# A two-block hybrid transformer on one core: transfer, rounding and subtraction of each piece of weights a thousand instructions ahead in the scheduler's order of preference

## The chip, the cores and the metric

The kernel runs on one core of a Trainium2 chip. The time is the device time of one execution in microseconds (us), lower is better; 2093.95 us is the median of three runs of the kernel before. The engines are named as in the profile: PE (TensorE, the matrix multiplier; PEld is its loading of the stationary operand), DVE (VectorE), ACT (ScalarE), POOL (GpSimd) and SP (SyncE, which here issues all the transfers of weights). Each engine executes its own instructions strictly in the order in which the program lists them.

## What is computed

A sequence of 256 tokens of width 1024 goes through a first block of two layers and a second block of one; everything is float32 and the batch is 1. Cut to what matters:

```python
def first_block(x, mem, ...):
    for l in range(2):
        x = x + 0.5 * swiglu(rms_norm(x, ffn1_norm[l]), ffn1_w_in[l], ffn1_w_out[l])
        z = rms_norm(x, mix_norm[l]) @ mix_w_in[l]      # Fox, MoBA and RWKV-7 heads
        y = concat([fox_mixer(z_fox), rwkv7_mixer(z_rwkv), moba_mixer(z_moba)])
        x = x + y @ mix_w_out[l]
        x = x + memory_cross_attention(rms_norm(x, ...), rms_norm(mem, ...), ...)
        x = x + 0.5 * swiglu(rms_norm(x, ffn2_norm[l]), ffn2_w_in[l], ffn2_w_out[l])
    return x

def second_block(x, c, ctx, ...):
    sh1, sc1, g1, sh2, sc2, g2 = split(silu(c) @ w_mod + b_mod, 6)
    p = modulate(rms_norm(x), sh1, sc1) @ w_in           # attention, delta rule, gates
    attn = latent_attention(q, [k_ctx, k], [v_ctx, v])
    gdn = gated_delta_rule_both_directions(ctx, x)       # solves triangular systems by chunk
    x = x + g1 * (merge(attn, gdn) @ w_out)
    x = x + g2 * conv_ffn(modulate(rms_norm(x), sh2, sc2), w_up, conv_w, conv_b, w_down)
    return rms_norm(x, final_norm_w)
```

The inner width of the FFNs is 2816. Nearly all bytes read are weights, each used once.

## The kernel before, in words

**Pieces of weights.** A product with weights is made from pieces of 128 x 1024 float32 numbers, 512 KB each. `piece` (L383) makes one: `raw` (L373) has SP issue the transfer (L375) into one of four `raw` buffers; ScalarE rounds it to the multiplier's format into `wh` (its instruction has L324, `act`), and VectorE subtracts to get the rest, `wl` = raw - wh (L327, `tt`). `wh` and `wl` have three buffers each. Activations are split in the same way, `xTh` and `xTl`, and PE adds up three products for one: xh.wh + xl.wh + xh.wl (L351, `mm`), 24 matmuls of 256 columns to a piece where the activations are stationary or moving in that width. There are 546 pieces.

**Who uses them.** `gemm_tok` (L403) and `gemm_chan` (L434, called in pairs by `gemm_pair`, L446) take a piece right before the matmuls that use it; `mix_out` (L855) does so for the mixers' output. A flag and a queue in `turn` let one product go after another.

**The order of the work.** The program is written as generators that yield estimated times (`merge`, L204ff; `START`, `PACE`), which sets the order in which instructions are handed to a scheduler. The scheduler then lists each engine's instructions by its own estimate of when their operands are ready; among those that are ready the earlier in the program has preference. `high_priority(offset=n)` shifts this preference of the enclosed instructions n instructions forward. Buffers still have to come free: a new `wh` waits until PE has read the third one before it.

**Stages.** A first FFN (with the modulation of block 2's vectors and the cross-attention's keys as side work: sums `macc`, loads `wm`), mixer 0, cross-attention 0, FFN, FFN (with block 2's context as side work), mixer 1, cross-attention 1 and FFN (again with modulation), then block 2: projections, the delta rule in four head groups and attention, the merge, and the convolution FFN. In the mixers and in the delta rule `inverse` (L676) inverts unit triangular matrices of 128: VectorE shuffles (L701) into `iv_tz`, a loop of 15 products `iv_p` and sums `iv_x`, masks into `gW`, `rW` or `iv_tz` and transposes (L720), then PE and ScalarE steps. The delta rule's next group waits for the inverse of the one before (`inv0`, `inv1`, ...). `gcv` are the sums of its short convolution; each reads a PSUM bank that a product has filled.

**The start.** `Builder.__init__` issues the four quarters of `x` (L295), the identity (the first 128 columns of `fconst`, L297) and the first norm's gains (`prm`, L298). PE transposes `x` with the identity (L354), ScalarE and VectorE split it into `xTh` and `xTl`, and the first product begins.

Of the kernel before, what the change touches and what calls it, by code (L numbers as in the profile page):

```python
# [10 lines left out]
F32 = mybir.dt.float32  # L11
F32R = mybir.dt.float32r
# [15 lines left out]
START = (7.0, 9.0, 29.0, 9.0, 85.0, 15.0, 47.0)  # L28

PACE = (2.2, 2.7)  # L30

WM = 4

# [242 lines left out]
class Builder:  # L276
# [104 lines left out]
        s.ts(out, out, 0.5, 0.5, OP.mult, OP.add)  # L381

    def piece(s, src, n):  # L383
        r = s.raw(src, n)
        h = s.stage.tile([128, 1024], F32R, name="wh", bufs=3)
        l = s.stage.tile([128, 1024], F32R, name="wl", bufs=3)
        s.act(h[:, :n], r[:, :n])
        s.sub(l[:, :n], r[:, :n], h[:, :n].bitcast(F32))
        return h, l

    def turn(s):
# [1159 lines left out]
    def gdn_group(s, e, ec, X, hp, latent, S, o, flags, spare):  # L1551
# [56 lines left out]
        def inv():  # L1608
# [30 lines left out]
            a.update(W=W, DT=DT)  # L1639
            yield from s.inverse(e, N, W, (True, False), (1.0, 1.0) if latent else PACE)  # L1640
            flags.add(f"inv{hp}")
# [457 lines left out]
```

## Time and profile before

| | |
|---|---|
| three runs | 2092.67, 2093.95, 2097.84 us |
| the profiled execution | 2097.77 us, of which 2095.9 us are the profile's span |
| PE busy | 2006.1 us (96%) |
| DVE busy | 1604.1 us (77%) |
| ACT busy | 1113.9 us (53%) |
| mean granted clock of PE | 0.974 of full speed |
| transfers | 317.16 MB, mean 151 GB/s |

PE's busy time counts a matmul from its start to its modelled end, so 96% does not mean that it runs at its peak. The idle time of an engine is put down to what released the instruction that ended it, its releaser. Where the granted clock is under 1, matmuls of a stretch ran partly at the lower of the two levels, 1.2 instead of 2.4 GHz.

### The profile page before, as it was taken

How to read it: one execution, taken by the hardware profiler on the slowest of the kernel's cores; microseconds unless marked ns; L12 is line 12 of the kernel's file. 1: busy time of each engine (PE TensorE's matmuls, PEld its weight loads, DVE VectorE, ACT ScalarE, POOL GpSimd, SP SyncE). 2: the span in 40 equal slices, each digit the busy share in tenths (PEclk: the TensorE clock that was granted, in tenths of full speed). 3: DMA queues.
4: the chain of work that ended last, by engine and by line, in shares of the span. 5: the costliest groups of instructions: out<-in, count | busy, mean ns of one | idle time of the engine just before them, and what ended most of it. 6: DMA issues, size and time to landing. Idle time of an engine off the chain costs nothing.

```text
span 2095.9 us, 37277 instructions
## 1 busy us (share of the span) xinstructions
PE 2006.1 (96%) x14344; PEld 1778.8 (85%) x14344; DVE 1604.1 (77%) x3828; ACT 1113.9 (53%) x2057; POOL 14.9 (1%) x16
## 2 busy tenths in 40 slices
PE   8999999999999999999999979999889999999998
PEld 8899878778989889898888758999678888878996
DVE  7978688677786969686787678766688887767985
ACT  6544555476455555464554354444546664546663
POOL 0000000000000000000000000000000000000000
PEclk9999999999999999999988988999989999999999
DMA  8775432154554545554432167665431123554663
GB/s 296 243 231 174 154 113 90 54 172 133 171 160 152 154 148 160 153 164 145 150 111 71 44 234 245 210 193 173 140 111 61 51 62 110 174 168 163 194 194 126
DMA packets 90568, 317.16 MB, mean 151 GB/s; under 512 B 10388, under 2 KB 12952, under 8 KB 90008
## 3 DMA queue, kind: packets, MB, share of 16 engines
q1 hardware_dynamic: 90392, 314.80, 47.5%
q8 instruction: 112, 1.84, 0.4%
q14 instruction: 64, 0.52, 0.1%
HBM read 313.72 MB, written 1.05 MB: 150 GB/s over the span
## 4 chain that ended last, share of the span: by engine, by line
PE 77%; DVE 16%; ACT 4%; issue 2%; DMA 0%; SPq 0%; DVEq 0%; ACTq 0%
PE b L351 73%; DVE wl L327 4%; PE b L354 3%; ACT wh L324 1%; DVE iv_x L348 1%; DVE iv_tz L701 1%; DVE iv_p L327 1%; DVE macc L345 1%; DVE gcv L345 1%; DVE sg L327 1%; ACT sq L324 1%; ACT iv_c L324 0%; DVE iv_tz L327 0%; DVE sg L345 0%; ACT fcb L324 0%
## 5 line engine op out<-in xcount | busy, mean ns | idle before, releaser
L324 ACT ACTIVATE wh<-raw 128x1024 fp32r<-128x1024 f32 (+1 forms) x546 | 569.0, 1043 | 604.4 <-PE b L351 443.2
L327 DVE TENSOR_TENSOR wl<-raw,wh 128x1024 fp32r<-128x1024 f32 (+1 forms) x546 | 654.6, 1204 | 262.3 <-ACT wh L324 241.2
L351 PE MATMUL b<-xTh,wh 128*128 128x256 f32 x2200 | 627.8, 286 | 2.9 <-ACT xTh L324 2.7
L351 PE MATMUL b<-xTh,wl 128*128 128x256 f32 x2200 | 621.9, 283 | 2.1 <-DVE xTl L345 1.2
L351 PE MATMUL b<-xTl,wh 128*128 128x256 f32 x2200 | 621.5, 283 | 0.2
L351 PEld LDWEIGHTS b<-xTh,wh 128*128 128x128 f32 x2200 | 418.2, 190 | 8.7 <-ACT xTh L324 4.5
L351 PEld LDWEIGHTS b<-xTh,wl 128*128 128x128 f32 x2200 | 418.8, 190 | 4.5 <-DVE wl L327 1.6
L351 PEld LDWEIGHTS b<-xTl,wh 128*128 128x128 f32 x2200 | 419.5, 191 | 2.9 <-DVE xTl L345 0.7
L351 PE MATMUL b<-wh,gh 128*128 128x512 f32 x440 | 175.9, 400 | 0.2 <-DVE gcv L345 0.2
L351 PE MATMUL b<-wl,gh 128*128 128x512 f32 x440 | 173.4, 394 | 0.1
L351 PE MATMUL b<-wh,gl 128*128 128x512 f32 x440 | 173.4, 394 | 0.0
L351 PE MATMUL b<-wh,xTh 128*128 128x512 f32 x400 | 161.6, 409 | 7.4 <-DVE iv_x L348 5.0
L351 PE MATMUL b<-wh,xTl 128*128 128x512 f32 x400 | 162.6, 406 | 0.0
L351 PE MATMUL b<-wl,xTh 128*128 128x512 f32 x400 | 159.9, 401 | 1.3 <-DVE wl L327 1.3
L351 PEld LDWEIGHTS b<-wl,gh 128*128 128x128 f32 x440 | 83.2, 189 | 19.0 <-DVE wl L327 0.6
L351 PEld LDWEIGHTS b<-wh,xTh 128*128 128x128 f32 x400 | 75.8, 191 | 27.6 <-issue 7.7
L351 PEld LDWEIGHTS b<-wh,gh 128*128 128x128 f32 x440 | 83.3, 189 | 18.2 <-ACT wh L324 0.6
L351 PEld LDWEIGHTS b<-wh,gl 128*128 128x128 f32 x440 | 83.3, 189 | 17.1
L351 PEld LDWEIGHTS b<-wl,xTh 128*128 128x128 f32 x400 | 76.3, 191 | 17.8 <-DVE wl L327 2.3
L351 PEld LDWEIGHTS b<-wh,xTl 128*128 128x128 f32 x400 | 76.6, 191 | 16.5 <-issue 2.3
L345 DVE SCALAR_TENSOR_TENSOR macc<-wm,mcs,macc 128x512 f32<-128x512 f32 x112 | 82.4, 744 | 0.3
L324 ACT ACTIVATE iv_tz<-b 128x256 f32<-128x256 f32 (+3 forms) x52 | 19.7, 380 | 66.0 <-PE b L351 65.7
(609 smaller groups left out, 3107.1 us busy)
## 6 DMA issues: line engine op xcount, KB each, us to landing
raw<-in_f1i_dram SPq DMA_DIRECT2D x88, 512.0 KB, 4.0
raw<-in_f2i_dram SPq DMA_DIRECT2D x88, 512.0 KB, 4.0
wm<-in_wmod_dram SPq DMA_DIRECT2D x48, 512.0 KB, 4.7
raw<-in_wup_dram SPq DMA_DIRECT2D x44, 512.0 KB, 4.3
raw<-in_f1o_dram SPq DMA_DIRECT2D x40, 512.0 KB, 3.6
raw<-in_wi_q_dram SPq DMA_DIRECT2D x40, 512.0 KB, 3.9
raw<-in_f2o_dram SPq DMA_DIRECT2D x40, 512.0 KB, 3.6
raw<-in_wi_a_dram SPq DMA_DIRECT2D x32, 512.0 KB, 3.9
```

The lines of the kernel that those rows point to most:

```text
L324: return s.nc.scalar.activation(out, in_, func, scale=scale, bias=bias, **kw)
L327: return s.nc.vector.tensor_tensor(out, a, b, op=op)
L345: return s.nc.vector.scalar_tensor_tensor(out, a, sc, b, op0=op0, op1=op1)
L348: s.nc.vector.tensor_reduce(out, in_, axis=AX.X, op=op)
L351: s.last_mm = s.nc.tensor.matmul(out, lhsT, rhs, start=start, stop=stop).ins
L354: s.nc.tensor.transpose(out, in_, s.c("ident"))
L701: nc.vector.stream_shuffle(AR[:, j, :, j:], NC[:, :, j:], [j] * 16 + [16 + j] * 16)
```

## The change

Transfer, rounding and subtraction of a piece are put in a block with a preference of 1000 instructions. What is computed and the buffers stay the same; lines behind the new ones move by two (up to `piece`) and by four (behind it).

```diff
 PACE = (2.2, 2.7)
+
+AHEAD = 1000
...
     def piece(s, src, n):
-        r = s.raw(src, n)
-        h = s.stage.tile([128, 1024], F32R, name="wh", bufs=3)
-        l = s.stage.tile([128, 1024], F32R, name="wl", bufs=3)
-        s.act(h[:, :n], r[:, :n])
-        s.sub(l[:, :n], r[:, :n], h[:, :n].bitcast(F32))
+
+        with s.tc.high_priority(offset=AHEAD):
+            r = s.raw(src, n)
+            h = s.stage.tile([128, 1024], F32R, name="wh", bufs=3)
+            l = s.stage.tile([128, 1024], F32R, name="wl", bufs=3)
+            s.act(h[:, :n], r[:, :n])
+            s.sub(l[:, :n], r[:, :n], h[:, :n].bitcast(F32))
         return h, l
```

SP's queue at the start of the program; `raw` are the pieces, `x` the input, the first `fconst` the identity, the first `prm` the first norm's gains. Before:

```order
L295 DMA x<-in_x_dram 128x512 x2
L297 DMA fconst<-in_fconst_dram 128x128
L298 DMA prm<-in_prm_dram 128x8
L295 DMA x<-in_x_dram 128x512 x2
L375 DMA raw<-in_f1i_dram 128x1024 x5
L301 DMA fconst<-in_fconst_dram 128x1318
L375 DMA raw<-in_f1i_dram 128x1024
L302 DMA prm<-in_prm_dram 128x510
L305 DMA uraw<-in_uconst_dram 128x1024
L307 DMA pos_i<-in_pos_dram 128x2
```

With the change:

```order
L377 DMA raw<-in_f1i_dram 128x1024 x4
L297 DMA x<-in_x_dram 128x512
L377 DMA raw<-in_f1i_dram 128x1024 x3
L297 DMA x<-in_x_dram 128x512
L299 DMA fconst<-in_fconst_dram 128x128
L300 DMA prm<-in_prm_dram 128x8
L297 DMA x<-in_x_dram 128x512 x2
L303 DMA fconst<-in_fconst_dram 128x1318
L304 DMA prm<-in_prm_dram 128x510
L307 DMA uraw<-in_uconst_dram 128x1024
```

Seven pieces now stand ahead of the identity and of three of the four quarters of `x`. Pieces need one of four `raw` buffers, so the fifth to seventh are issued when the first to third have been subtracted.

VectorE's order in block 2, in the inverse of the first head group; the shuffles are the rows `iv_tz<-iv_n`, `wl` the subtraction of a piece. Before, the last ten shuffles and the loop's beginning:

```order
L701 STREAM_SHUFFLE iv_tz<-iv_n 128x8x12
L701 STREAM_SHUFFLE iv_tz<-iv_n 128x8x11
L701 STREAM_SHUFFLE iv_tz<-iv_n 128x8x10
L701 STREAM_SHUFFLE iv_tz<-iv_n 128x8x9
L701 STREAM_SHUFFLE iv_tz<-iv_n 128x8x8
L701 STREAM_SHUFFLE iv_tz<-iv_n 128x8x7
L701 STREAM_SHUFFLE iv_tz<-iv_n 128x8x6
L701 STREAM_SHUFFLE iv_tz<-iv_n 128x8x5
L701 STREAM_SHUFFLE iv_tz<-iv_n 128x8x4
L701 STREAM_SHUFFLE iv_tz<-iv_n 128x8x3
L701 STREAM_SHUFFLE iv_tz<-iv_n 128x8x2
L327 TENSOR_TENSOR iv_p<-iv_tz,iv_x 128x16
```

With the change, from the seventh shuffle on:

```order
L329 TENSOR_TENSOR wl<-raw,wh 128x1024
L705 STREAM_SHUFFLE iv_tz<-iv_n 128x8x10
L705 STREAM_SHUFFLE iv_tz<-iv_n 128x8x9
L705 STREAM_SHUFFLE iv_tz<-iv_n 128x8x8
L705 STREAM_SHUFFLE iv_tz<-iv_n 128x8x7
L705 STREAM_SHUFFLE iv_tz<-iv_n 128x8x6
L705 STREAM_SHUFFLE iv_tz<-iv_n 128x8x5
L329 TENSOR_TENSOR wl<-raw,wh 128x1024
L705 STREAM_SHUFFLE iv_tz<-iv_n 128x8x4
L705 STREAM_SHUFFLE iv_tz<-iv_n 128x8x3
L329 TENSOR_TENSOR wl<-raw,wh 128x1024
L705 STREAM_SHUFFLE iv_tz<-iv_n 128x8x2
```

Three subtractions stand among the shuffles where none stood before, and the `gcv` that followed the loop's first product now stands ahead of all shuffles. Counted to the end of this inverse's loop, seven more subtractions stand ahead than before. In each mixer up to four more stand ahead of the end of the first inverse's loop; by the end of each of these stages the count is the same again. In the FFNs the subtractions keep their places among the FFN's own work, but the first FFN's 28 first modulation sums `macc` stand five to eight subtractions earlier.

## Rows read from the trace of the kernel before

**Rows 1.** The page's busy shares, and its chain that ended last, by line

```profile
PE 2006.1 (96%) x14344; PEld 1778.8 (85%) x14344; DVE 1604.1 (77%) x3828; ACT 1113.9 (53%) x2057; POOL 14.9 (1%) x16
...
PE b L351 73%; DVE wl L327 4%; PE b L354 3%; ACT wh L324 1%; DVE iv_x L348 1%; DVE iv_tz L701 1%; DVE iv_p L327 1%; DVE macc L345 1%; DVE gcv L345 1%; DVE sg L327 1%; ACT sq L324 1%; ACT iv_c L324 0%; DVE iv_tz L327 0%; DVE sg L345 0%; ACT fcb L324 0%
```

**Rows 2.** The page's costliest groups: pieces and modulation sums

```profile
L324 ACT ACTIVATE wh<-raw 128x1024 fp32r<-128x1024 f32 (+1 forms) x546 | 569.0, 1043 | 604.4 <-PE b L351 443.2
L327 DVE TENSOR_TENSOR wl<-raw,wh 128x1024 fp32r<-128x1024 f32 (+1 forms) x546 | 654.6, 1204 | 262.3 <-ACT wh L324 241.2
...
L345 DVE SCALAR_TENSOR_TENSOR macc<-wm,mcs,macc 128x512 f32<-128x512 f32 x112 | 82.4, 744 | 0.3
```

**Rows 3.** List of waits (waiter <- releaser: us in total, times, longest us)

```profile
ACT wh L324 <- PE b L351: 443.2, 340, 4.2
...
DVE wl L327 <- ACT wh L324: 241.2, 237, 6.7
...
PE b L351 <- DVE iv_tz L327: 10.2, 6, 3.3
...
PE b L351 <- DVE iv_tz L720: 6.9, 4, 2.2
...
PE b L351 <- DVE iv_x L348: 5.8, 3, 5.0
...
PE b L351 <- DVE wl L327: 2.1, 4, 1.1
```

**Rows 4.** Timeline, 0 to 22 us (start, us, engine, line, operation)

```profile
0.73 0.86 SPq L295 DMA_DIRECT2D x<-in_x_dram  x2
...
3.53 8.76 SPq L375 DMA_DIRECT2D raw<-in_f1i_dram  x5
3.63 0.63 ACT L324 ACTIVATE sq<-x 128x512 f32<-128x512 f32 x1 [1.62 <-DMA x<-in_x_dram]
...
5.38 1.94 PE L354 MATMUL b<-fconst,x 128*128 128x128 f32 x8 [5.38 <-DMA fconst<-in_fconst_dram]
...
9.62 1.06 ACT L324 ACTIVATE wh<-raw 128x1024 fp32r<-128x1024 f32 x1 [0.33 <-DMA raw<-in_f1i_dram]
...
10.71 1.22 DVE L327 TENSOR_TENSOR wl<-raw,wh 128x1024 fp32r<-128x1024 f32 x1 [0.26 <-ACT wh L324]
...
10.80 0.56 PE L351 MATMUL b<-xTh,wh 128*128 128x256 f32 x1
...
11.98 0.58 PE L351 MATMUL b<-xTh,wl 128*128 128x256 f32 x1 [0.41 <-DVE wl L327]
...
16.43 0.28 PE L351 MATMUL b<-xTh,wh 128*128 128x256 f32 x1
...
16.55 0.28 PE L351 MATMUL b<-xTl,wh 128*128 128x256 f32 x1
```

**Rows 5.** Transfers, 0 to 15 us (GB/s in 40 slices; issues, KB, us to landing)

```profile
GB/s 0 0 0 0 66 289 257 339 341 211 87 178 205 316 246 289 311 339 311 251 235 251 350 404 437 404 426 426 404 448 350 229 98 66 142 142 306 393 442 398
...
fconst<-in_fconst_dram SPq DMA_DIRECT2D x1, 64.0 KB, 3.6
```

**Rows 6.** Busy time by stretch: us, PE, PEld, DVE, ACT, POOL, PEclk, DMA share, GB/s

```profile
62.00:100.00 38.00, 37.84 (x240) 34.00 (x241) 37.35 (x68) 21.76 (x33) 0.00 (x0) 1.00 0.72 229
...
312.00:425.00 113.00, 110.35 (x862) 85.17 (x861) 81.95 (x240) 55.24 (x127) 3.72 (x3) 0.99 0.23 72
...
1090.00:1215.00 125.00, 122.65 (x917) 96.81 (x916) 83.79 (x246) 56.09 (x128) 3.71 (x3) 0.91 0.20 64
1485.00:1560.00 75.00, 66.19 (x373) 55.47 (x373) 63.62 (x206) 41.60 (x83) 0.00 (x0) 0.92 0.42 132
1560.00:1760.00 200.00, 188.99 (x1575) 170.58 (x1576) 170.09 (x599) 115.52 (x274) 0.00 (x0) 0.96 0.21 65
```

**Rows 7.** Timeline of TensorE, 1530 to 1560 us

```profile
1543.16 0.76 PE L351 MATMUL b<-wh,xTh 128*128 128x512 f32 x1 [4.96 <-DVE iv_x L348]
```

**Rows 8.** Timeline of VectorE, 1530 to 1560 us

```profile
1542.54 0.47 DVE L345 SCALAR_TENSOR_TENSOR gcv<-b,prm,gcv 128x255 f32<-128x255 f32 x1
```

## The prediction

> **What bounds the kernel now.** I read the busy shares first: TensorE (PE) is busy 2006.1 of 2095.9 us, and 73% of the chain that ended last is line 351, the matmuls [rows 1]. So only about 90 us are not PE, and a change of order can touch those alone, or the granted clock. Next the makers of a piece. ScalarE's 546 roundings (`wh`) and VectorE's 546 subtractions (`wl`) cost 1.04 and 1.20 us each [rows 2]. In the list of waits, the roundings wait on PE 340 times for 443.2 us in all: they wait for one of the three `wh` slots to be read. The subtractions then wait for the roundings, 241.2 us. PE in turn waits for a subtraction 4 times, 2.1 us in all [rows 3]. The reader is to see that the pieces are already as early as their buffers allow wherever PE is the bound. PE's longer waits go back to the inverse's small VectorE operations: 10.2, 6.9 and 5.8 us, 22.9 us in sum [rows 3]. Last I read the first 22 us in order of time [rows 4], the transfers there [rows 5], and the busy time by stage [rows 6].
>
> **The change, part by part.** Nothing is added or removed; instructions change places on their queues.
>
> *Start-up.* Before, SP issues `x`, `ident` (in `fconst`) and `prm` first and the pieces from 3.53 us on [rows 4]. Now seven pieces stand ahead of the second quarter of `x` and of `fconst`, without which PE can transpose nothing. Pieces 5 to 7 need a `raw` slot, so the seventh is issued when the third `wl` has ended. The first piece is issued where `x` was, at 0.73 us. The square of `x` started at 3.63 us, 2.9 us after `x` was issued [rows 4]; the piece has twice the bytes (about 0.6 us more at the 400 GB/s that the transfer row reaches [rows 5]), so the first `wh` starts near 3.5 to 4.2 us, and three `wl` behind it (1.06 + 3 x 1.22 us [rows 4]) end near 8.1 to 8.9. I take 8.2; `x` is issued at about 8.6 and `fconst` 0.4 us behind. At the 3.6 us from issue to landing that `fconst` shows [rows 5], the transposes start near 12.7 us, where before they began at 5.38 [rows 4]. Before, the first weight matmul ran at 10.80 us [rows 4], held by the first `wh` (9.62 + 1.06 us); now the pieces lie ready, and from transposes to matmul there are only some 2 us (eight transposes take 1.94 us [rows 4]): 14.7. That is 3.9 us later. The wait for the first `wl`, 0.4 us [rows 4], goes; the second eight transposes, which ran while PE waited, now add about half of the 1.94 us that eight take, 1.0. Sum: **+4.5 us**. Bounds: 2.5 if the second transposes stay hidden and the transfers land 1 us earlier, 8.6 if the whole 7.3 us stay and the last half of `x`, 0.5 MB, adds 1.3. The transfers moved past (the 659-KB rest of `fconst`, `prm`, `uraw`, `mem`) come before piece 8; seven pieces of 24 matmuls at 0.12 us from start to start [rows 4], 2.8 us each, cover them with some 20 us, so I cost them at nothing; without that cover they would cost PE the transfer itself, 0.66 MB at 400 GB/s, 1.7 us.
>
> *First FFN.* There the modulation's 28 first sums (`macc`, 744 ns [rows 2]) stand 5 to 8 pieces earlier on VectorE than before, because the pieces' order against the side work has shifted. VectorE is busy 37.35 of 38 us between 62 and 100 us, yet PE 37.84 [rows 6]. Taken as nothing, since PE has up to three subtracted pieces, 8.4 us, in store; the bound is eight sums, 6 us.
>
> *Weights waited for.* PE's 2.1 us behind `wl` [rows 3] should go: **-2.1 us**, at the utmost.
>
> *Chains delayed.* VectorE works in order. A `wl` put in front of the inverse's steps costs 1.2 us of that chain, and what waits behind it on VectorE are shuffles, products and the transposes that PE needs next. By the order, VectorE has up to 4 more `wl` ahead of the end of the first inverse in each mixer and 7 more in block 2; by the end of each stage the count is level again. So 4 x 1.2 = 4.8 us, twice, and 8.4 us. But the same `wl` are missing later, where the chain's next steps find VectorE emptier. Only what VectorE was idle there is not given back: in the later stretches it is busy 81.95 of 113, 83.79 of 125 and 170.09 of 200 us [rows 6], idle 27, 33 and 15%. That makes 1.3 + 1.6 + 1.3 = **+4.2 us**. Bounds: 0 (PE is fed by the pulled-forward matmuls and never sees the delay) and 18 (nothing comes back).
>
> **Sum:** 4.5 + 4.2 - 2.1 = +6.6 us against the profiled execution's own 2097.77, which is 3.8 us above the median shown: 2104.4. On the median, 2093.95 + 6.6 = **2100.5 us**.
>
> **Rivals.**
>
> *Faster: filler closes the waits in the chain.* The matmuls of the pieces move as well: in block 2 PE has up to 5.9 pieces more ahead of the first inverse's end, in the mixers up to 2.75. PE is in order too. At 1543.16 us it had idled 4.96 us for a convolution matmul [rows 7] whose releaser, a `gcv` sum, stood behind all shuffles on VectorE and ran only at 1542.54 [rows 8]; now the `gcv` sums stand ahead of the shuffles. If such matmuls run while the inverse works, and the inverse is not the later end of its stage, half of the 22.9 us goes: 2093.95 + 4.5 - 2.1 - 11.5 = 2085; with all of it 2073. The granted clock would go the same way: it is 0.92 in 1485 to 1560 us and 0.91 in 1090 to 1215 [rows 6], so up to 5 and 11 us lie there. It decides once the filled waits exceed the 4.5 us of the start. Against it: what is pulled forward is missing at the end of the stage, where PE waits for the inverse again (188.99 of 200 us busy in 1560 to 1760 [rows 6]). The Trainium skill ("Perfetto Trace Analysis", Matmul Optimizations) says the matmul engine scales its power with its utilization, and wants matmuls back to back in batches; by that rule each filled wait would raise the clock as well. The trace agrees in part: the clock is 0.92 where PE idles 8.8 of 75 us, but 0.91 also where it idles 2.4 of 125 [rows 6].
>
> *Slower by more: the chain keeps its delay.* If all `wl` pulled forward lie on the chain that ends the stage, and PE has no filler left behind it: 4.5 + 18 = +22.5, 2116.5. For it: block 2's inverse has the four head groups one behind another, so a delay of the first runs through. Against it: VectorE is 73, 67 and 85% busy later, so it does regain.
>
> *No effect: the slots decide.* The order of preference moves a piece only as far as `wh` and `wl` slots come free, and those wait on PE 443.2 us [rows 3]. Then the start's lag is taken up by the first FFN's waits, the mixers' gains and losses cancel, and the time is 2091 to 2097, say 2094. The Trainium skill ("Perfetto Trace Analysis", Optimization Strategy) reads a gap that repeats through a kernel as a possible lack of buffers; by that rule it would be the slot count, not the order, that limits. Rows 3 agree for ScalarE, which is not the engine that bounds. Against it: the order shows real moves in the mixers, block 2 and at the start.
>
> **How the numbers follow.** My forecast's own case 0.44 (2096 to 2106, from the lower bounds of its terms to their middle), faster 0.22 (2073 to 2088), much slower 0.15 (2110 to 2119), no effect 0.19. A measurement of this kernel can tell about 0.3% from no change, 6.3 us: 2087.7 to 2100.2. Slower by more is half of the forecast's case and the much slower one, 0.22 + 0.15, with a little from the first-FFN bound: 0.39. Faster by more is 0.22. The rest, 0.39, is the same. The range leaves out the lower third of the faster case and the upper part of the much slower one: 2081 to 2114.
>
> **What would show it.** At the start: the first transposes near 12.7 us and the first weight matmul near 14.7; if PE starts weight matmuls before 12, the start's term is wrong. In the list of waits: PE behind `wl` near 0, the roundings' wait on PE still above 400 us, and PE's wait behind `iv_x` at the first inverse of block 2 gone while waits behind `iv_tz` and behind the transposes grow. If the mixers and block 2 as stages become shorter by more than 5 us in sum, the term of the delayed chains has the wrong sign and the faster rival holds; if PE's busy share in the first 100 us falls by more than the start's 4.5 us, the pulled-forward `macc` sums were not covered.

## The result and the profile after

The changed kernel took 2128.89 us in the median of 4 runs (2112.36 to 2134.99) beside 2094.32 for the kernel before (4 runs, 2092.67 to 2097.84): a ratio of 1.0155 with an interval of 1.0112 to 1.0198. It is slower, as forecast, but by five times as much as forecast: 35 us, not 6.6, and above the range's 2114. The profiled execution took 2134.99 us, its span is 2133.1 us, and the mean granted clock of TensorE in it is 0.961, where that of before is 0.974. One run of one kernel below (2144.44 us, everything except mixers and block 2, at a clock of 0.960) lies more than 1.5% above the fastest of its kernel and is left out of its figures.

The page of the changed kernel: busy shares, the chain that ended last by line, and the makers of a piece.

```profile
PE 2030.8 (95%) x14344; PEld 1790.3 (84%) x14344; DVE 1611.0 (76%) x3828; ACT 1115.9 (52%) x2057; POOL 14.8 (1%) x16
...
PE b L353 71%; DVE wl L329 6%; PE b L356 4%; ACT wh L326 2%; DVE iv_x L350 1%; DVE macc L347 1%; DVE iv_tz L705 1%; DVE iv_p L329 1%; ACT iv_c L326 1%; DVE gcv L347 1%; DVE sg L329 0%; ACT sq L326 0%; DVE sg L347 0%; DVE gl L329 0%; DMA raw<-in_f1i_dram 0%
...
L326 ACT ACTIVATE wh<-raw 128x1024 fp32r<-128x1024 f32 (+1 forms) x546 | 569.5, 1044 | 618.5 <-PE b L353 447.6
L329 DVE TENSOR_TENSOR wl<-raw,wh 128x1024 fp32r<-128x1024 f32 (+1 forms) x546 | 654.9, 1202 | 275.0 <-ACT wh L326 254.1
```

Beside [rows 1] PE is busy for 24.7 us more with the same 14344 matmuls. So of the 37.2 us by which the span grew, only about 12 are PE's idle time: matmuls themselves became longer. A piece costs its makers what it did [rows 2]; its share of the chain went from 4% to 6% at the subtraction, and PE's own line from 73% to 71%.

The list of waits of the changed kernel (waiter <- releaser: us in total, times, longest us):

```profile
ACT wh L326 <- PE b L353: 447.6, 342, 5.9
...
PE b L356 <- DMA fconst<-in_fconst_dram: 16.2, 1, 16.2
...
PE b L353 <- DVE iv_tz L724: 12.3, 7, 2.9
...
PE b L353 <- DVE macc L347: 9.4, 4, 5.8
...
PE b L353 <- DVE iv_tz L329: 2.8, 3, 1.1
```

PE's 2.1 us behind `wl` [rows 3] are gone, and so are the 5.8 us behind `iv_x`; the roundings still wait for PE, 447.6 us. Behind the masks and transposes `iv_tz` PE waits 12.3 and 2.8 us where before it waited 6.9 and 10.2 [rows 3]: in sum a little less, where the prediction had both grow. The wait behind the identity at the start has grown from 5.4 [rows 4] to 16.2 us, and that behind `macc`, the modulation's sums, from 5.5 to 9.4.

Timeline of the changed kernel, 0 to 24 us (start, us, engine, line, operation; beside [rows 4]):

```profile
0.73 1.80 SPq L377 DMA_DIRECT2D raw<-in_f1i_dram  x4
...
5.42 2.45 DVE L329 TENSOR_TENSOR wl<-raw,wh 128x1024 fp32r<-128x1024 f32 x2 [5.42 <-ACT wh L326]
...
6.68 3.52 SPq L377 DMA_DIRECT2D raw<-in_f1i_dram  x3
...
8.62 1.23 DVE L329 TENSOR_TENSOR wl<-raw,wh 128x1024 fp32r<-128x1024 f32 x1 [0.74 <-ACT wh L326]
...
10.25 0.43 SPq L297 DMA_DIRECT2D x<-in_x_dram  x1
10.73 0.42 SPq L299 DMA_DIRECT2D fconst<-in_fconst_dram  x1
...
16.16 1.97 PE L356 MATMUL b<-fconst,x 128*128 128x128 f32 x8 [16.16 <-DMA fconst<-in_fconst_dram]
...
17.84 0.58 PE L353 MATMUL b<-xTh,wh 128*128 128x256 f32 x1
```

SP stands at 6.68 us with the fifth piece, waits for buffers until 10.20, and issues the identity only at 10.73. It lands 5.4 us later. The first weight matmul runs at 17.84 us, 7.0 us later than before.

The time by stage. A stage ends here with VectorE's update of `x`. First FFN, 0 to 142.9 and 142.9 to 239.2 us; first mixer; the two FFNs beside which the context's work runs; second mixer; cross-attention 1; block 2. Columns: us, busy us of PE, PEld, DVE, ACT and POOL (instructions), granted clock, DMA share, GB/s. The changed kernel:

```profile
0.00:142.90 142.90, 125.10 (x828) 114.08 (x829) 111.74 (x212) 76.38 (x114) 0.20 (x4) 1.00 0.74 245
142.90:239.20 96.30, 96.30 (x707) 90.72 (x706) 70.77 (x113) 43.88 (x64) 0.05 (x1) 1.00 0.60 190
239.20:452.10 212.90, 205.78 (x1434) 162.98 (x1432) 156.81 (x456) 107.50 (x228) 7.26 (x6) 0.94 0.31 98
513.10:1037.40 524.30, 510.03 (x4048) 473.44 (x4047) 398.38 (x948) 272.66 (x504) 0.05 (x1) 0.98 0.49 153
1037.40:1263.10 225.70, 216.46 (x1433) 175.45 (x1432) 157.42 (x460) 106.72 (x227) 7.27 (x6) 0.88 0.29 92
1263.10:1327.30 64.20, 48.55 (x210) 39.16 (x209) 54.79 (x117) 27.50 (x57) 0.00 (x0) 0.79 0.76 255
1517.90:1933.80 415.90, 389.78 (x2692) 332.93 (x2692) 332.04 (x966) 229.21 (x466) 0.00 (x0) 0.97 0.35 110
```

The same stages of the kernel before:

```profile
0.00:135.30 135.30, 126.33 (x819) 115.33 (x820) 110.54 (x211) 74.97 (x114) 0.20 (x4) 1.00 0.77 257
135.30:232.70 97.40, 97.40 (x717) 91.81 (x716) 71.89 (x113) 44.35 (x65) 0.05 (x1) 1.00 0.61 190
232.70:436.60 203.90, 195.37 (x1434) 158.51 (x1432) 154.65 (x456) 106.44 (x228) 7.26 (x6) 0.99 0.32 103
497.50:1015.10 517.60, 504.42 (x4048) 469.47 (x4047) 396.94 (x947) 273.62 (x504) 0.00 (x0) 0.99 0.50 155
1015.10:1227.80 212.70, 206.71 (x1435) 168.29 (x1433) 156.44 (x462) 106.41 (x227) 7.36 (x6) 0.94 0.31 99
1227.80:1288.50 60.70, 46.42 (x206) 37.89 (x205) 52.58 (x114) 27.15 (x56) 0.00 (x0) 0.80 0.78 255
1479.00:1898.00 419.00, 391.59 (x2692) 336.30 (x2692) 330.22 (x967) 229.00 (x467) 0.00 (x0) 0.96 0.35 110
```

The differences: first FFN +6.5, first mixer +9.0, the two context FFNs +6.7, second mixer +13.0, cross-attention 1 +3.5, block 2 -3.1; stages not in the list +1.6. That is the 37.2 us. In the mixers the number of matmuls is the same (1434 and 1434, 1435 and 1433) while PE's busy time grew by 10.4 and 9.8 us and the clock fell from 0.99 to 0.94 and from 0.94 to 0.88. Time by clock of the two mixers together is 212.9 x 0.94 + 225.7 x 0.88 = 399 after and 203.9 x 0.99 + 212.7 x 0.94 = 402 before. At the same clock the mixers cost no more than they did.

A stretch of the first mixer of the changed kernel in which the clock is low, same columns:

```profile
392.00:408.00 16.00, 16.00 (x51) 9.88 (x50) 7.46 (x38) 2.91 (x5) 0.00 (x0) 0.50 0.00 1
```

The same place of the kernel before, which reaches it 14 us earlier:

```profile
378.00:394.00 16.00, 16.00 (x87) 11.16 (x87) 10.80 (x30) 7.40 (x11) 0.00 (x0) 1.00 0.19 56
```

Before, these 16 us hold 87 matmuls, 11 ScalarE operations and a DMA share of 0.19: pieces are still being made between the inverse's steps. After, they hold 51 matmuls, 5 ScalarE operations and a DMA share of 0.00, and TensorE runs at a clock of 0.50, its lower level (1.2 GHz of 2.4), for all 16 us. It is tempting to read the second from the first: pieces pulled forward leave a thin stretch, and the thin stretch is clocked lower. But PE is busy for all of the 16 us in both, so fewer matmuls are also what half the clock makes of the same work, and these two rows do not tell which comes first. The runs with the mixers below bear on it.

The first inverse of block 2, VectorE's timeline: the product that ends its loop. After:

```profile
1612.29 1.09 DVE L329 TENSOR_TENSOR gW<-iv_x,fconst 128x512 f32<-128x512 f32 x1
```

Before:

```profile
1559.20 1.08 DVE L327 TENSOR_TENSOR gW<-iv_x,fconst 128x512 f32<-128x512 f32 x1
```

From the stage's start (1517.9 and 1479.0 us) that is 94.4 us after and 80.2 before: the chain is 14.2 us later. The stretch from the inverse's first operation on VectorE to this product (columns as by stage), after and before:

```profile
1580.10:1612.29 32.19, 29.69 (x221) 27.53 (x220) 32.00 (x112) 20.13 (x35) 0.00 (x0) 1.00 0.48 155
```

```profile
1539.14:1559.20 20.06, 16.04 (x89) 14.16 (x89) 19.37 (x75) 10.11 (x14) 0.00 (x0) 0.83 0.35 108
```

VectorE is busy for 32.00 of 32.19 us, and was for 19.37 of 20.06: the delay is its own work. Ten subtractions stand in the stretch where four stood, 12.2 us of them instead of 4.9, and the other 5 us or so are convolution sums, rotations and the like of products that PE now makes earlier. The remaining 2.1 of the 14.2 us lie ahead of the inverse. Yet the stage ends 3.1 us sooner.

### The profile page after: what moved, and what is told of

It reads as the page before. It is cut to its first block, busy times and chain, and to the rows that moved or that the text cites. A ratio compares the mean times of both kernels' runs of the same rounds, so it can differ in the third digit from the quotient of the medians.

```text
span 2133.1 us, 37352 instructions
## 1 busy us (share of the span) xinstructions
PE 2030.8 (95%) x14344; PEld 1790.3 (84%) x14344; DVE 1611.0 (76%) x3828; ACT 1115.9 (52%) x2057; POOL 14.8 (1%) x16
## 4 chain that ended last, share of the span: by engine, by line
PE 75%; DVE 16%; ACT 5%; issue 3%; DMA 1%; SPq 0%; ACTq 0%; DVEq 0%
PE b L353 71%; DVE wl L329 6%; PE b L356 4%; ACT wh L326 2%; DVE iv_x L350 1%; DVE macc L347 1%; DVE iv_tz L705 1%; DVE iv_p L329 1%; ACT iv_c L326 1%; DVE gcv L347 1%; DVE sg L329 0%; ACT sq L326 0%; DVE sg L347 0%; DVE gl L329 0%; DMA raw<-in_f1i_dram 0%
## 5 line engine op out<-in xcount | busy, mean ns | idle before, releaser
L326 ACT ACTIVATE wh<-raw 128x1024 fp32r<-128x1024 f32 (+1 forms) x546 | 569.5, 1044 | 618.5 <-PE b L353 447.6
L350 DVE TENSOR_REDUCE iv_x<-iv_p 128x8 f32<-128x16 f32 (+4 forms) x180 | 51.3, 285 | 2.2
```

The lines of the kernel that those rows point to most:

```text
L326: return s.nc.scalar.activation(out, in_, func, scale=scale, bias=bias, **kw)
L350: s.nc.vector.tensor_reduce(out, in_, axis=AX.X, op=op)
```

## The experiments

In all but three of the twelve (the transfers alone, the preference of 100 and the changed kernel once more) the switch below turns the change on in some stages alone; what each edits is where `ahead` is true. Differences of a mean are against the kernel before on the same chip or beside it; of all its runs on those chips the means are 2094 to 2097 us and the mean clocks 0.9755 to 0.9772.

```diff
-        with s.tc.high_priority(offset=AHEAD):
+        with s.tc.high_priority(offset=AHEAD) if s.ahead else nullcontext():
```

**The transfers alone.** Rounding and subtraction are put back in their old order.

```diff
         with s.tc.high_priority(offset=AHEAD):
             r = s.raw(src, n)
+        if True:
             h = s.stage.tile([128, 1024], F32R, name="wh", bufs=3)
```

> Only the transfer of a piece has the preference; rounding and subtraction keep theirs. The order then differs from the kernel before in the first 46 pieces alone: eight pieces' transfers ahead of most of the input at the start, and the first modulation loads and sums some six pieces earlier. Start theory: the first transposes of TensorE come near 16 us and the first product near 18 us as in the changed kernel, and 5 to 9 us of this are left at the end: 2099 to 2103 us. Rival, the first FFN absorbs it: 2092 to 2097 us. The prediction's term was +4.5: 2098.5 us.

Measured: 2107.1 us in the median of 10 runs (2088.55 to 2118.97), 1.0034 [0.9994, 1.0074]; the mean is 9.1 us above before's and the clock 0.9768, as before's. The first eight transposes start here:

```profile
15.88 1.97 PE L356 MATMUL b<-fconst,x 128*128 128x128 f32 x8 [15.88 <-DMA x<-in_x_dram]
17.56 0.58 PE L353 MATMUL b<-xTh,wh 128*128 128x256 f32 x1
```

The whole lag of the start is there with the transfers alone: the first weight matmul is 6.8 us later than before, and the first half of the first FFN ends at 143.3 us, 8.0 later. The modulation's sums stand as early on VectorE here as with the whole change (the first one behind 4 subtractions, before behind 11), so by its end time this kernel does not separate them from the queue; but the lag is there at the first weight matmul already, ahead of all of them.

**The first FFN alone** (with its side work):

```diff
-        s.late = None
+        s.late, s.ahead = None, True
...
+        s.ahead = False
         s.run(s.mixer(0))
```

> The whole preference (transfer, rounding and subtraction) in the first FFN and its side work alone. If only the pieces' transfers ahead of the input matter there: as with the transfer alone, +9 us by the mean of the runs, first FFN 240 to 241 us, 2103 us. If rounding and subtraction add to it (the parts measured alone sum to 24 us, the whole change costs 33): +14 us or more, 2109 us.

Measured: 2099.67 us (12 runs, 2091.27 to 2111.65), 1.0029 [1.0007, 1.0052], mean +6.2 us, clock 0.9774 beside 0.9769. Transposes start at 16.63 us, and the first FFN's two halves take 239.6 us, 6.9 more than before's 232.7. No clock is lost.

**The whole change, with `x`, identity and gains put first again**, and the preference off during cross-attention 1:

```diff
+            with s.tc.high_priority(offset=(10 - 4 * hf) * AHEAD):
                 for tb in range(2):
                     s.nc.sync.dma_start(s.x[:, tb, hf * 512:hf * 512 + 512], xin[:, tb, hf * 512:hf * 512 + 512])
...
+            s.ahead = False
             s.run(s.xattn(1, s.p("n2_1")), side)
+            s.ahead = True
```

> The changed kernel with two repairs: the input, the identity and the first gains are issued ahead of all pieces, and the cross-attention of layer 1 keeps the old order (no preference there). The part theory (the start costs 8 us, a modulation sum that TensorE meets in the cross-attention of layer 1 costs 5 us, the mixers cost granted clock): the first product at about 11 us, the first FFN within 1 us of the kernel before (233 us), the cross-attention 61 to 62 us instead of 66, and 2128.9 - 13 = 2112 to 2118 us in all. Rival (the loss is spread and follows from the order of everything): over 2122 us. Faster rival (what is left of the preference pays): below 2094 us.

Measured: 2116.59 us (10 runs, 2098.06 to 2129.22), 1.0085 [1.0048, 1.0122], mean +21.6 us, clock 0.9673 beside 0.9766.

```profile
11.07 0.58 PE L354 MATMUL b<-xTh,wh 128*128 128x256 f32 x1 [0.82 <-ACT wh L327]
```

The start is repaired: the first weight matmul comes at 11.07 us where it came at 17.84 (10.80 before). The stage is repaired by half: the first FFN takes 236.1 us, 3.4 more than before's 232.7, where I expected it within 1. PE waits in it 3.1 us behind `sXl`, a split of the side work, and 2.6 behind `xTl`, where before has 1.4 and none; which moved instructions do that was not tested. Cross-attention 1 takes 61.9 us. Against the whole change some 12 us of the mean are won back, 5 of them in these two stages by the profiles (239.2 to 236.1 and 64.2 to 61.9), and most of the clock's loss stays, 0.0093 of 0.0117. That splits the cost in two: a smaller part at places that can be named, and the clock.

**Cross-attention 1 and the FFN behind it alone:**

```diff
+            s.ahead = True
             s.run(s.xattn(1, s.p("n2_1")), side)
             s.run(s.ffn(d["f2i_1"], d["f2o_1"], None), side)
             s.hold = False
             side.drain()
+            s.ahead = False
```

> The preference in cross-attention 1 and the FFN behind it alone; the order differs in one point on TensorE, the closing of one modulation sum some 33 pieces earlier, and in its sums on VectorE. From the stages: cross-attention 1 at 64 to 65 us instead of 60.4 to 60.9, nothing else: +3.6 us, 2098 us. Rival (it is given back in the FFN behind, where the closing is now missing): within 1 us of the kernel before. If the parts add up, start (8), context (3 to 5) and this one (3.6) leave about 8 us of the 24 to the clock.

Measured: 2100.62 us (12 runs, 2095.18 to 2126.31), 1.0035 [1.0002, 1.0069], mean +5.9 us, clock 0.9747. Cross-attention 1 takes 64.0 us, as with the whole change (64.2) and not as before (60.7). PE's closes in it, the small products that end a modulation sum `macc`:

```profile
1243.05 0.98 PE L353 MATMUL b<-fconst,macc 128*128 128x2 f32 x4 [2.95 <-issue]
...
1251.35 1.05 PE L353 MATMUL b<-fconst,macc 128*128 128x2 f32 x8 [1.51 <-DVE macc L347]
1258.25 1.84 PE L353 MATMUL b<-fconst,macc 128*128 128x2 f32 x8 [5.84 <-DVE macc L347]
1268.96 1.40 PE L353 MATMUL b<-fconst,macc 128*128 128x2 f32 x8 [1.89 <-DVE macc L347]
...
1296.26 1.03 PE L353 MATMUL b<-fconst,macc 128*128 128x2 f32 x8 [0.20 <-DVE macc L347]
```

In the kernel before:

```profile
1240.68 0.95 PE L351 MATMUL b<-fconst,macc 128*128 128x2 f32 x8
...
1251.90 1.87 PE L351 MATMUL b<-fconst,macc 128*128 128x2 f32 x8 [5.26 <-DVE macc L345]
...
1268.89 1.87 PE L351 MATMUL b<-fconst,macc 128*128 128x2 f32 x8 [0.22 <-DVE macc L345]
...
1403.07 0.95 PE L351 MATMUL b<-fconst,macc 128*128 128x2 f32 x8
```

Eight closes lie between this stage's start and the end of the FFN behind it; the sixth is the last line of either list. It now stands 6 us behind this stage, where before it stands 115 us behind it, late in the FFN. The pieces' order has shifted against the side work on VectorE as well: ahead of the first close VectorE has five subtractions of this stage where before it had two. PE is in order, and at each close it stands until VectorE's `macc` is through. Its waits behind `macc` grew from 5.5 to 9.2 us, and the 2.95 us ahead of the first close, for which the list names no releaser, end as VectorE gets through the sums there. Other waits fell by nearly as much (behind `xP` from 6.9 to 2.2 us, behind `xqT` from 1.8 to none): PE is idle for 15.7 us of the stage where before it was for 14.3, and busy for 48.4 where it was for 46.4. That is the stage's +3.3. With the whole change but the preference off in this stage (the kernel above) the closes wait 5.26 and 0.22 us, as before.

**The two FFNs with the context's work alone:**

```diff
+            s.ahead = True
             s.run(s.ffn(d["f2i_0"], d["f2o_0"], s.p("n1_1")), side)
             s.run(s.ffn(d["f1i_1"], d["f1o_1"], s.p("nm_1")), side)
             s.hold = False
             side.drain()
+            s.ahead = False
```

> The preference in the two FFNs between cross-attention 0 and mixer 1 alone, beside which block 2's context runs. From the stages of the earlier profiles (second of the two FFNs 256.3 to 256.8 us with the preference, 253.0 to 253.6 without; the first 264 to 268 in either): +3 to +5 us, 2098 to 2100 us. Clock rival (the preference in the FFNs lowers the granted clock of the whole run, since the excess of all parts but mixers and block 2 was 24 us by the mean of its runs and only 15 by the stages of its profile): +8 to +12 us and a mean clock below 0.974.

Measured: 2094.46 us (12 runs, 2087.12 to 2108.07), 0.999 [0.9955, 1.0024], mean -0.4 us, clock 0.9783. The time that I expected, 2098 to 2100 us, does not show. The profiled execution has these stages 8 us longer than before's, but its runs had on average a clock 0.0028 above before's, which by the 17 us for 0.01 that is worked out below hides some 4 or 5 us. So neither a cost nor its absence is shown here.

**The two mixers alone:**

```diff
+        s.ahead = True
         s.run(s.mixer(0))
+        s.ahead = False
...
+        s.ahead = True
         s.run(s.mixer(1))
+        s.ahead = False
```

> The preference holds in the two mixers alone. Chain theory (pieces pulled ahead on VectorE and TensorE delay the inverses, and nothing gives it back at the stage's end): +9 and +13 us in the two mixers as in the changed kernel's profile, 2110 to 2116 us, with the first inverse's end 5 us later and the later stretches at a lower granted clock. Rival (the mixers' loss is a consequence of the late start or of the clock's state before them): no change, 2090 to 2098 us. The prediction's term was 1.3 + 1.6: 2097 us.

Measured: 2103.19 us (10 runs, 2091.8 to 2112.45), 1.0016 [0.9983, 1.005], mean +6.6 us, clock 0.9735 beside 0.9772. The late stretches of both mixers have the lower clock:

```profile
384.00:400.00 16.00, 16.00 (x64) 10.34 (x63) 6.87 (x29) 1.81 (x3) 0.52 (x1) 0.51 0.00 1
1176.00:1192.00 16.00, 16.00 (x109) 11.50 (x104) 3.20 (x7) 4.00 (x7) 1.38 (x1) 0.57 0.00 1
```

But other runs take the first mixer away from this reading. The kernels with the preference in the context's FFNs, in cross-attention 1 and in block 2 alone have the order of the kernel before in the first mixer (on VectorE and ScalarE it is the same instruction by instruction, on PE but for four matmuls). Their first mixers, in this order, and a late stretch of the first of them:

```profile
232.10:454.22 222.12, 213.72 (x1434) 172.76 (x1432) 154.84 (x457) 106.39 (x228) 7.27 (x6) 0.90 0.30 95
231.43:446.75 215.32, 207.10 (x1434) 168.85 (x1432) 154.79 (x457) 106.37 (x228) 7.26 (x6) 0.93 0.30 97
232.29:446.66 214.37, 205.84 (x1434) 168.14 (x1432) 154.79 (x456) 106.43 (x228) 7.27 (x6) 0.94 0.31 98
...
388.00:404.00 16.00, 16.00 (x52) 10.20 (x53) 5.24 (x17) 3.24 (x5) 0.00 (x0) 0.50 0.11 32
```

With the old order they took 214.4 to 222.1 us, more than the changed kernel's 212.9, and one of them has a late stretch of 16 us at 0.50 with 52 matmuls. Before's own 203.9 us was an execution with a high clock there. With the changed order the mixers-and-block-2 kernel below took

```profile
231.86:437.09 205.23, 198.01 (x1434) 158.40 (x1432) 156.81 (x456) 107.42 (x228) 7.26 (x6) 0.98 0.32 103
```

So the +9.0 us of the first mixer lie within the clock's spread from execution to execution and are not shown to be the order's: over all the profiles the first mixer takes 211.0 us in the mean of five with the preference of 1000 in it (the whole change twice, repaired, the mixers alone, mixers and block 2) and 211.8 us in the mean of seven with the old order. The second mixer takes 207.3 to 225.8 us in those five, in the mean 217.5, and 202.3 to 215.4 in those seven, in the mean 207.9: there a loss by the order is likely.

**Block 2 alone** (`ahead` true before `s.run(s.block2(out))`, nowhere else):

```diff
+        s.ahead = True
         s.run(s.block2(out))
```

> The preference holds in block 2 alone. From the changed kernel's profile (the first inverse of block 2 ends 14 us later, the stage's end comes 3 us earlier): 2088 to 2094 us. The prediction's delayed chain: +1.3 to +8.4 us, 2095 to 2103 us. The faster rival: up to 10 us less, 2084 us.

Measured: 2098.9 us (10 runs, 2088.24 to 2107.7), 1.0004 [0.9976, 1.0032], mean +2.8 us, clock 0.9732 beside 0.9772: no difference in time that the runs can tell, though at a lower clock.

**Both mixers and block 2** (the edits of the last two together):

> The preference in both mixers and in block 2, nowhere else. If the parts add up: 6.6 (mixers alone) + 2.8 (block 2 alone) by the means of their runs = +9 us, 2105 us, mean clock 0.970. Rival (the loss of granted clock grows with the number of changed stages, which would explain why the repaired kernel of the second experiment batch still lost 21 us): +15 us or more, 2110 us, mean clock below 0.968.

Measured: 2103.63 us (12 runs, 2092.8 to 2113.25), 1.0047 [1.0018, 1.0076], mean +9.0 us, clock 0.9704 beside 0.9770. Mean time by mean clock is 2040.8 here and 2045.9 before: all of the 9.0 us, and more, is the clock. The delays of the chains cost nothing at an equal clock.

**The mixers again, with dense matmuls in the emptied stretches.** Eight more matmuls (their result is overwritten) ahead of each of the last five banks of a mixer's second inverse, 40 in a mixer, so that PE has work there as it had before. Added to the mixers-alone kernel:

```diff
+        def dense(ps):
+            if fill:
+                for _ in range(8):
+                    s.mm(ps[:, :256], s.X[0][:, 4, :128], s.X[0][:, 4])
+            return ps
...
-        ps = e.bank()
+        ps = dense(e.bank())
```

> The preference in the mixers alone, and in the last five steps of the second inverse of each mixer eight more matmuls of 256 columns per step, whose result the step's own matmuls overwrite: 40 per mixer, at 0.12 us from start to start 4.7 us of TensorE per mixer if nothing else changes, so +9 us on the mixers alone, 2112 us. Sparse theory (with the pieces pulled ahead, TensorE has little dense work left there and its granted clock falls to half): no half-clock stretch of 12 to 16 us in the second inverse, so some 6 us come back per mixer, 2098 to 2106 us. Rival (the clock falls for another reason): the half-clock stretch about 150 to 165 us after the mixer's start stays, 2110 to 2118 us.

Measured: 2105.04 us (10 runs, 2086.57 to 2115.35), 1.0038 [0.9991, 1.0084], mean +8.4 us, clock 0.9754 beside 0.9766; the mixers alone had +6.6 us, and 0.9735 beside 0.9772, with 80 matmuls fewer.

```profile
384.00:400.00 16.00, 16.00 (x114) 11.81 (x113) 11.08 (x40) 4.51 (x8) 0.65 (x1) 1.00 0.04 12
1176.00:1192.00 16.00, 15.81 (x92) 11.04 (x91) 6.39 (x21) 2.41 (x4) 1.01 (x1) 0.77 0.03 9
```

In the first mixer the stretch is at a clock of 1.00 where the mixers alone had 0.51; in the second, 1176 to 1192 us are at 0.77 where they had 0.57. The median fits the first of the two theories. But the changed kernel, run once more below, has the first mixer's stretch at 1.00 without any added matmul, so one profile on either side does not show what the matmuls did. By the means they cost 1.8 us (8.4 against 6.6, on two chips), where 80 matmuls at the 0.12 us from start to start [rows 4] are 9.6 us of PE, and the clock is nearer to before's; neither difference is clear of the runs' spread. Whether emptied stretches cost clock stays open.

**Everything except mixers and block 2:**

```diff
-        s.late = None
+        s.late, s.ahead = None, True
...
+        s.ahead = False
         s.run(s.mixer(0))
+        s.ahead = True
```

(and the same around the second mixer; false ahead of block 2)

> The preference holds everywhere but in the mixers and block 2. If the FFNs with the context as side work (+6.5 us in the changed kernel's profile) and the cross-attention of layer 1 (+3.5) lose by the order as the start does (+6.5): 2108 to 2113 us. Rival, only the start counts and the other losses came from the mixers' lag or the clock: as with the transfer alone, 2098 to 2102 us. If the three parts add up, the excess of this one, of the mixers alone and of block 2 alone sum to the changed kernel's 34 us.

Measured: 2120.5 us (9 runs, 2100.58 to 2129.31), 1.01 [1.0059, 1.0142], mean +21.4 us, clock 0.9714 beside 0.9772. More than half of the whole is here, against what I expected, and again with a lower clock than before's. With the +9.0 us of mixers and block 2, measured on another chip, that is 30.4 of the whole change's 33.5 us.

**A preference of 100 in place of 1000:**

```diff
-AHEAD = 1000
+AHEAD = 100
```

> The whole change with a preference of 100 instead of 1000 instructions. At the start three pieces instead of seven stand ahead of the input; the mixers' and block 2's pieces move little, the modulation sum of the cross-attention of layer 1 as far as with 1000. Part theory: start +3 to +5 us, cross-attention +5, the context's FFNs +2 to +3, mixers and block 2 as before: 2104 to 2108 us. Rival (only a long reach hurts): 2094 to 2098 us.

Measured: 2110.07 us (10 runs, 2093.16 to 2115.89), 1.0057 [1.0021, 1.0092], mean +12.8 us, clock 0.9715 beside 0.9766. The first FFN takes 235.9 us and cross-attention 1 takes 61.2: the named places cost half or less, and the clock still falls. Neither size of the preference beats the kernel before.

**The changed kernel once more**, unedited, on the chip of the mixers-and-block-2 kernel:

> The changed kernel itself once more, beside the kernel before on one chip, since its first four runs spread over 22 us: the parts measured alone sum to 9.1 (start) - 0.4 (context) + 6.0 (cross-attention 1) + 6.6 + 2.8 = +24 us, 2118 us; by the first four runs it is +32 to +34, 2127 us. Time less the clock's loss (time x clock) should lie 5 to 9 us above the kernel before, as in the first runs; the rest is granted clock.

Measured: 2131.0 us (6 runs, 2115.22 to 2136.41), 1.0158 [1.0112, 1.0204], mean +33.5 us, clock 0.9653 beside 0.9770. Its profiled execution of 2115.22 us has, in the first mixer and in the second:

```profile
392.00:408.00 16.00, 16.00 (x102) 10.77 (x102) 12.30 (x50) 4.44 (x7) 0.68 (x1) 1.00 0.03 11
1176.00:1192.00 16.00, 16.00 (x130) 11.25 (x123) 3.67 (x8) 4.08 (x9) 1.38 (x1) 0.57 0.00 1
```

The same kernel has the first mixer's stretch at 0.50 in one execution and at 1.00 in another, with 51 and 102 matmuls in 16 us and a DMA share of 0.00 and 0.03. So a stretch with hardly a piece in it can run at full clock, and the halved number of matmuls goes with the clock.

**What the runs add up to.** The whole costs 33.5 us of mean. Mean time by mean clock is 2053.8 for it and 2045.9 before, 7.9: divided by before's clock of 0.977 that is 8 us at an equal clock and 25 of clock. By the kernel before itself, whose runs reach from 2084.18 us at a clock of 0.983 to 2115.03 at 0.965, 0.01 of clock is 17 us, and the 0.0117 lost are 20. So 20 to 25 us are clock and 8 to 13 are work that ends later.

The parts' means sum to 6.2 (first FFN) - 0.4 (context) + 5.9 (cross-attention and FFN) + 9.0 (mixers and block 2) = 20.7 us, 12.8 less than the whole. Taken at an equal clock, an estimate with the 17 us for 0.01, the parts are 7.0 + 4.4 + 4.4 - 2.2 = 13.6 us and the whole is 33.5 - 20 = 13.5: the work that ends later adds up, and stands in the first FFN (the start above all), in cross-attention 1 and the FFN behind it and, as far as these runs can tell, in the context's FFNs, while mixers and block 2 give a little back. What does not add up is the clock: the parts change it by +0.0005, +0.0028, -0.0009 and -0.0066, the whole by -0.0117. Two readings stay open. The parts' intervals, their half-widths added in squares, are 0.0061 of the ratio wide to either side, 13 us, so chance in the clocks may be all of it. Or the clock falls further when several stages are changed at once: the kernel with everything except mixers and block 2 lost 0.0058, though its three parts alone lost no more than 0.0009. (Cross-attention 0, the one stage of it that no part has, takes 61.0 us with the whole change and 60.9 before.) These runs do not tell the two apart.

## Why the prediction was wrong in size

The prediction's sign was right, and the start that it priced does cost time. It failed because the largest cost was not a term of its sum: the granted clock. That its terms sum to 6.6, near the 5 us that the places they stand for cost at an equal clock (7.0 for the first FFN, -2.2 for mixers and block 2), is luck: one was too small and the other had the wrong sign.

*Start-up: right in kind, mis-sized.* The forecast was +4.5 us, with transposes at 12.7 and the first weight matmul at 14.7. They came at 16.16 and 17.84, and the first FFN was 6.2 (its own mean) to 6.9 us longer: within the bound of 8.6. Two steps failed. "`x` is issued at about 8.6" was 10.25, since the third subtraction did not end at 8.2 but at 9.85: its rounding waited for a piece behind the first two. And "at the 3.6 us from issue to landing" was 5.4: that row [rows 5] is of an identity issued ahead of the pieces, and this one stood behind three of them. The transfers-alone kernel shows that it is the queue; putting `x` first again gives back the lag of the first matmul, and half of the stage's.

*First FFN's early sums: nothing, as forecast.* The lag is 7.0 us at the first weight matmul and 6.5 at the end of the first FFN, so nothing was added to it. That the moved work is free there by itself is not shown: with the start repaired 3.4 us stay.

*Weights waited for: right.* PE's waits behind `wl` are gone, 2.1 us.

*Delayed chains: right in kind, wrong at both ends.* The first inverse of block 2 is 14.2 us later, not 8.4: the subtractions were counted, but the products pulled forward bring other work on VectorE ahead of the inverse's steps as well, some 5 us of it. And all of it comes back by the stage's end, where the forecast kept the idle share of VectorE, +4.2 us: at an equal clock mixers and block 2 together cost nothing, by the estimate above -2.2.

*What was not in the sum: the clock.* The prediction begins with "a change of order can touch those alone, or the granted clock", but its sum puts the clock at nothing, and gives no reason. "The granted clock would go the same way" stands in the faster rival alone, where filled waits were to raise it by 5 and 11 us. That is the step that failed: the mean clock fell from 0.9770 to 0.9653, and 20 to 25 of the 33.5 us are that. Why it falls stays open. The prediction noted that "what is pulled forward is missing at the end of the stage" and priced it as idle time of PE; that it is paid in clock instead would fit the second mixer, and the first mixer speaks against it. By the Trainium skill ("Perfetto Trace Analysis", Matmul Optimizations) the engine's power follows its utilization, and matmuls should come in dense batches. In the prediction I let that rule speak for the change, from the waits that are filled, and not against it, from the stretches that are emptied. No run here shows that emptying does it: the late stretch of the first mixer ran at 0.50 and at 1.00 with the changed order, and at 0.50 and at 1.00 with the old one.

*What was not looked for: side work.* In cross-attention 1 subtractions came to stand ahead of the modulation's sums, and a close moved up from late in the last FFN, of which the prediction says nothing; +3.3 to +3.5 us.

*The rivals.* The faster one fell in time, though its 4.96 us wait [rows 7] did go, and the list of waits has none like it at that inverse. In block 2 it may have been half right: the stage is 3.1 us shorter in the profile, and block 2 alone, 2.8 us slower at a clock 0.0040 lower, is some 4 us faster at an equal clock by the same 17 us for 0.01. But its clock went down, not up. "Much slower" was nearest in time (2116.5), for a reason that did not hold: the chain does not keep its delay. "No effect" was right that the roundings go on waiting for PE (447.6 us) and wrong to conclude that the order then does not matter.

## What to carry to other kernels

A preference for prefetch moves whatever is in program order around it too: on an in-order issue queue the first input goes behind transfers that wait for buffers, and side work ends up among other instructions. Read the start of the queue and every stage's closes, not only the places that the change is for. Put the granted clock into the sum, if only as a bound: the runs of the kernel before, with their clocks, give its price before anything is changed (here 17 us for 0.01). Compare time by granted clock to see whether a stage does more work or the same work slower, and before blaming an order for a slow stretch, look for the same stretch in an execution that has the old order.

## What was not expected of the hardware

The mean granted clock of one and the same kernel on one core moves from run to run: of the kernel before from 0.965 to 0.983, with 2115.03 to 2084.18 us. The first mixer's stretch was at 0.50 in one execution of the changed kernel and at 1.00 in another, and first mixers with one and the same order took 203.9 to 222.1 us at clocks of 0.99 to 0.90. A reordering that leaves the number of matmuls as it is (14344) and PE's share at 95 to 96% changed the mean of these draws from 0.9770 to 0.9653, worth 20 to 25 us, more than all the work that it delayed; what in the order does that is not known.
